# Two-layer hybrid decoder trunk: tile arithmetic taken off GpSimd, constant products ahead of x, short transposes gathered

## The chip, the cores and the metric

The kernel runs on one core of a Trainium2 chip. The metric is device time in microseconds (us) of one execution; the median of several runs counts. TensorE (PE) does the matmuls and transposes, VectorE (DVE), ScalarE (ACT) and GpSimd (POOL) the elementwise work, SyncE (SP) issues most DMAs. PSUM is the accumulator memory that matmuls write to, SBUF the working memory that everything else lies in.

## The reference, cut to what matters

Two layers over a sequence of 512 rows and 1024 channels, all in fp32, then a last RMSNorm.

```python
for l in range(2):
    h = rmsnorm(x, g_mix[l]); z = h @ w_in[l]          # columns split among the three mixers and the gates
    a = swa_mixer(...)     # sliding window 128, 8 heads, rotary positions, a learned sink per head
    b = nsa_mixer(...)     # 8 heads; compressed, selected and windowed keys, gated per head
    c = mla_mixer(...)     # 8 heads; low-rank q and kv ("latent"), rotary part of 32 channels
    m = sum(sigmoid(gate_i) * (mixer_i @ w_br[l, i]))  # merge
    x = x + m @ w_out[l]
    x = x + cross_attention(rmsnorm(x, g_x[l]), mem)   # 4 heads of 128, 256 memory rows
    h = rmsnorm(x, g_ffn[l])
    x = x + (silu(h @ w_gate) * (h @ w_up)) @ w_d[l]   # inner size 2816
out = rmsnorm(x, g_final)
# rope(u) = u * cos + swap(u) * sin ; rmsnorm(x) = x / sqrt(mean(x^2) + eps) * g
```

## The kernel before, in words

Activations lie with channels on partitions: x is 8 tiles of 128x512 (channels x sequence). A product in fp32 accuracy is three matmuls of TensorE in a faster type: each operand is split into a high part and a rest, and `mm3` multiplies high by high (L307), rest of x by high of w (L308), high of x by rest of w (L309). For the weights, ACT writes the high part `wh` from the loaded `wraw` (L246) and DVE the rest `wl` (`tt`, L166). For the activations, `norm_split` has ACT write `xh` (L175) and DVE `xl` (L176), both already multiplied by the norm's gain. Weights come in chunks of 512 KB; SP issues their DMAs ahead of their use into three `wraw` buffers, POOL some of those of the FFN's combined weights (`sum`).

**A norm.** `norm_begin` names an engine; `norm_tile` squares a tile on ACT (L336) and adds it into `acc` on the named engine, GpSimd unless told otherwise. `norm_end` sums `acc` over partitions with matmuls onto ones (L359), adds a last part (`end`, L361), takes the root on ACT and the reciprocal on DVE, spreads the result over partitions with one more matmul (L371) and copies it from PSUM into `rstd` (L374). A norm's factor is applied behind the product that uses x, in `evac` or where the result is read (`tmp<-mm,rstd`), so the product's matmuls don't wait for it.

**Rotary positions.** `rotate` multiplies the swapped halves by `sin` on GpSimd, the tile by `cos` on DVE and adds. `k_tiles` then copies the two heads of a key tile out to both halves of the partitions: four copies on ACT, four subtractions on DVE.

**Attention.** A `Half` is two blocks of 128 queries of one head (four in mixer A). `attend` runs all of them as one pipeline of steps, one block a step: scores of the new block on PE, its softmax on DVE and ACT, and, four steps later (`lags`), `turn`: its block of probabilities is transposed on PE into a PSUM tile `tp`, and split into `ph` (ACT, L172) and `pl` (DVE, L173). When both blocks of a Half are turned, `values` multiplies with v into the one PSUM bank `av` (`av_tile`, one buffer), and one step later `out_half` empties the bank: ACT copies one half of its partitions (L701), DVE adds the other to it. The step's PE work is woven with matmuls of the projections by `skew`, `weave` and `drain`, and the order on each engine is then set by the framework's scheduler. DVE and ACT work strictly in that order.

**Merge, FFN, end.** `merge_tasks` multiplies each mixer's projection with its gate and adds the three into `mg` on GpSimd. In the FFN, `sums` forms the operands of a scheme with seven products in place of eight; two of its four differences are on GpSimd. `final` multiplies x by gain and norm in one DVE instruction for each of 16 half tiles (`fin`, L1450), and SP sends each out by a DMA of its own (L1452).

Of the kernel before, what the change touches and what calls it, by code (L numbers as in the profile page):

```python
# [121 lines left out]
CUTS, W1, POS, SQP = 2, 4, 5, (1, 2, 3, 4)  # L122
# [24 lines left out]
class Trunk:  # L147
    def __init__(self, ctx, tc, a, plan):
# [3 lines left out]
        self.lags = (2, 4)  # L152
# [169 lines left out]
    def norm_begin(self, n=512, eng=None, pool=None):  # L322
        return {"n": n, "acc": None, "x": [], "eng": eng or self.nc.gpsimd, "pool": pool or self.sh}
# [27 lines left out]
    def norm_end(self, st, dim, out, pool=None, bank=None):  # L351
# [5 lines left out]
        for j in range(nb):  # L357
            c = slice(j * 128, j * 128 + 128)
            nc.tensor.matmul(ps[:, j:j + 1], acc[:, c], self.ones[:, 0:1], start=True, stop="end" not in st)  # L359
            if "end" in st:  # L360
                nc.tensor.matmul(ps[:, j:j + 1], st["end"][:, c], self.ones[:, 0:1], start=False, stop=True)  # L361
# [11 lines left out]
        r = (pool or self.sh).tile([128, n], F32, name="rstd", tag="rstd", bufs=1 if pool else 2)  # L373
        nc.scalar.copy(r, ps)  # L374
        out["r"] = r
# [11 lines left out]
    def consts(self):  # L387
        nc, sh = self.nc, self.sh
        self.gains = sh.tile([128, G_FINAL + 8], F32, name="gains")
        nc.sync.dma_start(self.gains, self.a["gains"])  # L390
# [4 lines left out]
        nc.vector.memset(self.ones, 1.0)  # L395
        self.ident = sh.tile([128, 128], F32, name="ident")
# [93 lines left out]
    def k_tiles(self, kr):  # L490
# [45 lines left out]
    def k_task(self, src, x, n, box, key):  # L536
# [7 lines left out]
        box[key] = self.k_tiles(self.rotate(f, s))  # L544
# [11 lines left out]
    class Half:  # L556
# [3 lines left out]
        def __init__(self, o, scores, blocks, mask, scale, value, after, av=None, pre=None, last=True, init=3e38,  # L560
                     sink=False, gate=None, band=False):
            self.o, self.scores, self.blocks, self.mask, self.scale = o, scores, blocks, mask, scale
            self.value, self.after, self.av, self.pre, self.last = value, after, av, pre, last
            self.init, self.sink, self.gate, self.band = init, sink, gate, band
            self.ks = sorted(set(b for bl in blocks for b in bl))
            self.p, self.ps, self.ext = {}, {}, {}

# [35 lines left out]
        def turn(self, i):  # L603

            o, bl = self.o, self.blocks[i]
            if i == 0:
# [3 lines left out]
            if self.band:  # L610
                c = slice(bl[0] * 256 + 128 * (len(bl) - 1), i * 256 + 128)
                o.split(*(t.rearrange("p b q -> p (b q)")[:, c] for t in (self.ph, self.pl)),
                        tp.rearrange("p b q -> p (b q)"))
                return 110 * len(bl)
            j = self.ks.index(bl[0])
            c = slice(i * 128, i * 128 + 128)
            o.split(self.ph[:, j:j + len(bl), c], self.pl[:, j:j + len(bl), c], tp)
            return 110 * len(bl)

        def values(self):  # L620
# [4 lines left out]
            if "ps" not in self.av:  # L625
                self.av["ps"] = self.o.av_tile(512 if self.band else 256)
            ps = self.av["ps"]
            cost = 0
# [4 lines left out]
            elif self.pre is None and self.av.get("begun"):  # L633
                first = False
            self.av["begun"] = True
# [13 lines left out]
            todo = [(w, self.ks.index(b), c, x) for b, c in todo for w, x in self.value(self, b)]  # L649
            for n, (w, b, c, x) in enumerate(todo):  # L650
                nc.tensor.matmul(ps[:, c], w, x[:, b, c], start=first and n == 0,
                                 stop=self.last and n == len(todo) - 1)
            return cost + 109 * len(todo)

    def attend(self, jobs):

        q, done, out = [], [], []
        ls, lt = self.lags

        def step(new):  # L660
            cost = 0
            if new is not None:
                cost += new[0].score(new[1])
            if len(q) > ls and q[-ls] is not None:
# [3 lines left out]
            if len(q) > lt and q[-lt] is not None:  # L668
                h, i = q[-lt]
                cost += h.turn(i)  # L670
                if i == len(h.blocks) - 1:
                    done.append(h)
# [19 lines left out]
        for _ in range(lt + 3):  # L692
            yield step(None)

    def out_half(self, of, av, g, half, n=256):
# [3 lines left out]
        c = slice(256 * half, 256 * half + n)  # L699
# [8 lines left out]
    def jobs_a(self, l, box, of):  # L708
# [13 lines left out]
        for t in range(4):  # L722
            yield lambda t=t: ("q", t) in box
            of.append(self.of_tile())
            for g in range(2):
# [4 lines left out]
                                lambda ps, o=of[t], g=g: self.out_half(o, ps, g, 0, 512),  # L730
# [118 lines left out]
    def jobs_b(self, b, of):  # L849
# [18 lines left out]
        for t in range(4):  # L868
            yield lambda t=t: ("pc", t) in b and ("q", t) in b
            of.append(self.of_tile())  # L870
            for g in range(2):
                h = t + 4 * g
                for half in range(2):
                    av = {}
                    blocks = [list(range(i + 1)) for i in (2 * half, 2 * half + 1)]
                    for br, k, v in ((1, "ks", "vs"), (2, "kw", "vw")):
# [4 lines left out]
                                        lambda ps, o=of[t], g=g, half=half: self.out_half(o, ps, g, half), av=av,  # L881
                                        pre=(lambda ps, t=t, g=g, half=half: add_cmp(ps, t, g, half)) if br == 1 else None,
                                        last=br == 2, gate=gate)
# [93 lines left out]
    def jobs_c(self, box, of):  # L977
# [14 lines left out]
        for h in range(8):  # L992
# [3 lines left out]
            v = box[h][2]  # L996
            for half in range(2):
# [3 lines left out]
                                lambda ps, o=of[h // 2], g=h % 2, half=half: self.out_half(o, ps, g, half))  # L1001
# [585 lines left out]
```

## Time and profile before

| | |
|---|---|
| median of 3 runs | 2030.93 us (2027.62 to 2031.45) |
| profiled execution | 2028.9 us, its span 2027.2 us |
| PE busy | 1977.0 us, 98% |
| DVE / ACT / POOL busy | 1392.9 / 1196.9 / 243.2 us |
| mean granted TensorE clock | 0.996 of full speed |

How to read it: PE is busy nearly all the time, so the interesting figures are the short stretches in which it is not. A row of the timeline is one instruction or a run of equal ones: its start, its time, the engine, the line, and in square brackets how long the engine had been idle before it and whose result it then took up. A stretch in which PE's idle time is ended by DVE shows a wait for VectorE, and the next question is what VectorE did instead. The program's stages by time are: 0 to 50 us the loads and the first norm, 50 to 330 mixers A and B, 330 to 500 the latent mixer C, 500 to 650 merge and cross attention, 650 to 720 the entry of the FFN, up to 1005 the FFN; the second layer repeats this 1000 us later and ends with the last norm at 2016 to 2027.

### The profile page before, as it was taken

Reading aid. Unit: us, or ns where it says so; the run is one execution under the profiler, and the core shown is the slowest. Engines: PE = TensorE matmul, PEld = TensorE weight load, DVE = VectorE, ACT = ScalarE, POOL = GpSimd, SP = SyncE. Lnnn points to the kernel's source line nnn. Section 1 sums busy time; section 2 is a strip of 40 time slices with the busy share of each in tenths; the row PEclk is TensorE's granted clock in tenths of the full one; section 3 lists DMA queues with packets and bytes.
Section 4 is the critical chain, followed back from the end, with each engine's and each line's share of the span. In section 5 each row is a group of like instructions: output and inputs, shape, how many; then the busy total and the mean of one; then the engine's idle time right before and its main releaser. Section 6 shows DMA issues by size and latency. Waiting matters only on the chain. (4 is left out here: it accounts for less than half of the span.)

```text
span 2027.2 us, 30844 instructions
## 1 busy us (share of the span) xinstructions
PE 1977.0 (98%) x11368; PEld 1689.5 (83%) x11368; DVE 1392.9 (69%) x2734; ACT 1196.9 (59%) x2408; POOL 243.2 (12%) x234
## 2 busy tenths in 40 slices
PE   7999999999999999999999999999999999999998
PEld 5778887878888798989877788877788878989897
DVE  7897777676557884757577977676654579657475
ACT  5787786875456562534456867877744565435252
POOL 2210001012211200100112100001022021001000
PEclk9999999999999999999999999999999999999999
DMA  6321212224332563745343222122333344647432
GB/s 190 105 79 58 68 48 89 73 84 130 102 104 75 159 177 114 183 121 140 116 120 106 64 66 63 54 86 76 111 110 104 105 117 116 167 135 194 116 106 69
DMA packets 85743, 218.00 MB, mean 108 GB/s; under 512 B 11208, under 2 KB 17096, under 8 KB 85592
## 3 DMA queue, kind: packets, MB, share of 16 engines
q1 hardware_dynamic: 75800, 197.16, 31.5%
q0 software_dynamic: 9792, 18.88, 5.8%
q8 instruction: 89, 1.46, 0.3%
q14 instruction: 62, 0.51, 0.1%
HBM read 200.23 MB, written 4.75 MB: 101 GB/s over the span
## 5 line engine op out<-in xcount | busy, mean ns | idle before, releaser
L246 ACT CAST wh<-wraw 128x1024 fp32r<-128x1024 f32 (+3 forms) x275 | 277.4, 1009 | 367.5 <-PE mm L308 239.9
L307 PE MATMUL mm<-xh,wh 128*128 128x512 f32 x928 | 384.4, 414 | 7.8 <-ACT wh L246 6.5
L166 DVE TENSOR_TENSOR wl<-wraw,wh 128x1024 fp32r<-128x1024 f32 (+3 forms) x275 | 334.7, 1217 | 71.1 <-ACT wh L246 66.4
L308 PE MATMUL mm<-xl,wh 128*128 128x512 f32 x928 | 373.6, 403 | 3.8 <-DVE xl L176 3.8
L309 PE MATMUL mm<-xh,wl 128*128 128x512 f32 x928 | 371.7, 401 | 4.1 <-DVE wl L166 4.1
L309 PEld LDWEIGHTS mm<-xh,wl 128*128 128x128 f32 x928 | 176.0, 190 | 45.7 <-DVE wl L166 6.5
L307 PEld LDWEIGHTS mm<-xh,wh 128*128 128x128 f32 x928 | 176.7, 190 | 41.1 <-ACT wh L246 7.0
L308 PEld LDWEIGHTS mm<-xl,wh 128*128 128x128 f32 x928 | 177.0, 191 | 39.4 <-DVE xl L176 6.7
L589 ACT ACTIVATE p<-p,st 128x256 f32<-128x256 f32 (+5 forms) x288 | 155.3, 539 | 49.0 <-DVE st L583 42.8
L166 DVE TENSOR_TENSOR x<-x,mm 128x512 f32<-128x512 f32 (+1 forms) x88 | 55.6, 637 | 154.2 <-PE mm L309 153.9
L173 DVE TENSOR_TENSOR pl<-tp,ph 128x256 fp32r<-128x256 f32 (+3 forms) x288 | 131.2, 457 | 43.7 <-ACT ph L172 41.1
L601 ACT ACTIVATE p<-p,st 128x256 f32<-128x256 f32 (+3 forms) x288 | 141.8, 532 | 20.3 <-DVE st L166 12.8
L172 ACT CAST ph<-tp 128x256 fp32r<-128x256 f32 (+3 forms) x288 | 113.1, 395 | 40.0 <-PE tp L519 37.9
L583 DVE CUSTOM_DVE_ANT_0 p<-s,causal 128x128 f32<-128x128 f32 (+2 forms) x224 | 106.2, 476 | 39.6 <-PE s L859 16.1
L519 PE MATMUL tp<-ident,p 128*128 128x128 f32 x656 | 122.3, 278 | 8.3 <-DVE v L173 2.9
L166 POOL TENSOR_TENSOR acc<-acc,tmp 128x512 f32<-128x512 f32 (+1 forms) x55 | 75.6, 1375 | 450.3 <-ACT tmp L336 292.0
L308 PE MATMUL mm<-h,wh 128*128 128x512 f32 x304 | 120.2, 396 | 0.0
L307 PE MATMUL mm<-h,wh 128*128 128x512 f32 x304 | 120.2, 395 | 0.0
L309 PE MATMUL mm<-h,wl 128*128 128x512 f32 x304 | 120.2, 395 | 0.0
L519 PEld LDWEIGHTS tp<-ident,p 128*128 128x128 f32 x656 | 78.1, 141 | 31.0 <-DVE pl L173 6.9
L266 POOL DMA_DIRECT2D sum<-in_w_gu x36 | 43.7, 1239 | 455.9 <-DMA sum<-in_w_gu 205.7
L166 POOL TENSOR_TENSOR mg<-mg,gt 128x512 f32<-128x512 f32 x32 | 48.0, 1501 | 359.5 <-DVE gt L1040 359.3
(299 smaller groups left out, 4961.5 us busy)
## 6 DMA issues: line engine op xcount, KB each, us to landing
wraw<-in_w_in SPq DMA_DIRECT2D x91, 512.0 KB, 3.6
wraw<-in_w_gu SPq DMA_DIRECT2D x52, 512.0 KB, 3.6
sum<-in_w_gu SPq DMA_DIRECT2D x36, 512.0 KB, 4.6
sum<-in_w_gu POOLq DMA_DIRECT2D x36, 512.0 KB, 5.8
wraw<-in_w_d SPq DMA_DIRECT2D x32, 512.0 KB, 3.8
wraw<-in_w_br SPq DMA_DIRECT2D x24, 512.0 KB, 3.6
up<-in_w_gu SPq DMA_DIRECT2D x36, 256.0 KB, 2.7
wraw<-in_w_xkv SPq DMA_DIRECT2D x16, 512.0 KB, 3.5
```

Source lines behind the costliest of these rows:

```text
L166: (eng or self.nc.vector).tensor_tensor(out=out, in0=a, in1=b, op=op)
L172: nc.scalar.copy(hi, src)
L173: (eng or nc.vector).tensor_tensor(out=lo, in0=src, in1=hi.bitcast(F32), op=OP.subtract)
L246: nc.scalar.copy(wh[:, j:j + n], raw[:, j:j + n])
L266: nc.gpsimd.dma_start(s, ends, accum_op=OP.add)
L307: nc.tensor.matmul(ps, wh[:, c], xh, start=i == 0, stop=False)
L308: nc.tensor.matmul(ps, wh[:, c], xl, start=False, stop=False)
L309: nc.tensor.matmul(ps, wl[:, c], xh, start=False, stop=i == len(blocks) - 1)
L519: self.nc.tensor.transpose(tp[:, j], src[:, j * 128:j * 128 + 128], self.ident)
L583: o.nc.vector.tensor_tensor_reduce(out=p, in0=self.ps.pop(i), in1=self.mask(self.blocks[i]), scale=-self.scale, scalar=self.init, op0=OP.a ...
L589: self.o.nc.scalar.activation(p, p, AF.Exp, scale=-1.0, bias=st[:, 0, i:i + 1], accum_out=st[:, 1, i:i + 1])
L601: nc.scalar.activation(self.p[j], self.p[j], AF.Copy, scale=self.st[:, 2, j:j + 1])
```

## The change

- All tile arithmetic that POOL did (121 instructions: 41 and 14 additions into `acc` of 128x512 and 128x256, 32 additions into `mg`, 22 products with `sin`, 8 FFN differences, 4 squares) goes to DVE, the 4 squares to ACT. POOL keeps masks, fills, small sink copies and DMA issues.
- A turn gathers more: where the two blocks of a Half have at most four key blocks together (mixer A, the first halves of B and C, cross attention), both are transposed into one `tp` and split at once, three steps behind the second one's scores. 192 splits of 128 to 512 columns on each of ACT and DVE become 96 of 384 or 512.
- The two halves of a head in B, C and cross attention share one `av` bank, which is emptied once: 64 additions of 64x256 become 32 of 64x512, with as many copies.
- In two `k_tiles` per layer the second placement is done by two SP DMAs in place of two copies and two subtractions.
- In the final norm x times gain is done by ACT as soon as x is there; behind the norm stands one DVE product for two tiles, which reads the norm from PSUM without the copy, and 8 DMAs of two tiles instead of 16.
- At the start: 11 matmuls of ones ahead, the gains' DMA on ACT's queue, `positions` behind the last x, one weight chunk later.

```diff
+CUTS, W1, WARM = 2, 5, 11
-        self.lags = (2, 4)
+        self.lags = (2, 3, 4)
 def norm_begin
-        return {..., "eng": eng or self.nc.gpsimd, ...}
+        return {..., "eng": eng or self.nc.vector, ...}
 def norm_end
-        for j in range(nb):
-            nc.tensor.matmul(ps[:, j:j + 1], acc[:, c], self.ones[:, 0:1], start=True, stop="end" not in st)
-            if "end" in st:
-                nc.tensor.matmul(ps[:, j:j + 1], st["end"][:, c], ...)
+        parts = [acc] + ([st["end"]] if "end" in st else [])
+        for i, a in enumerate(parts):
+            for j in range(nb):
+                nc.tensor.matmul(ps[:, j:j + 1], a[:, j * 128:j * 128 + 128], self.ones[:, 0:1], ...)
...
-        nc.scalar.copy(r, ps)
+        if keep:
+            nc.scalar.copy(r, ps)
+            ps = r
 def rotate
-        self.tt(s, s, self.sin, OP.mult, self.nc.gpsimd)
+        self.tt(s, s, self.sin, OP.mult)
 def k_tiles
+        if copied:
+            for g, m in enumerate(halves):
+                self.tt(k[m, 2 + g], kr[m], k[m, g].bitcast(F32), OP.subtract)
+                nc.sync.dma_start(k[halves[1 - g], g::2].bitcast(F32), k[m, g::2].bitcast(F32))
+            return k
 class Half
+            self.paired = all(len(blocks[i]) + len(blocks[i + 1]) <= 4 for i in range(0, len(blocks), 2))
 def turn
-            tp = o.tp4(self.p.pop(i), len(bl))
+            todo = [(k, j) for j in ((i - 1, i) if self.paired else (i,)) for k in self.blocks[j]]
+            for n, (k, j) in enumerate(todo):
+                o.nc.tensor.transpose(tp[:, n], self.p[j][:, c:c + 128], o.ident)
...
+                o.split(... [:, c:c + 128 * n] ...)
 def values
-                self.av["ps"] = self.o.av_tile(512 if self.band else 256)
+                self.av["ps"] = self.o.av_tile(512)
+                ps = ps[:, 256 * self.half:256 * self.half + 256]
 def step
-            if len(q) > lt and q[-lt] is not None:
-                cost += h.turn(i)
+            if q[-lt] is not None and not q[-lt][0].paired:
+                cost += turn(*q[-lt])
+            if q[-lp] is not None and q[-lp][0].paired and q[-lp][1] % 2:
+                cost += turn(*q[-lp])
...
-            if done and not (len(q) > lt and q[-lt] is not None and q[-lt][0] is done[0]):
+            if done:
...
+            done.extend(fresh)
 def out_half
-        self.nc.scalar.copy(t[m, :n], av[x])
-        self.tt(of[m, c], av[m], t[m, :n], OP.add)
+        self.nc.scalar.copy(t[m], av[x])
+        self.tt(of[m], av[m], t[m], OP.add)
 def merge_tasks
-                self.tt(m, m, t, OP.add, nc.gpsimd)
+                self.tt(m, m, t, OP.add)
 def sums
-            self.tt(f[0], b11, b12, OP.subtract, nc.gpsimd)
-            self.tt(f[2], b22, b12, OP.subtract, nc.gpsimd)
+            self.tt(f[0], b11, b12, OP.subtract)
+            self.tt(f[2], b22, b12, OP.subtract)
 def down_half (last layer)
+            nc.scalar.activation(fins[-1][:, i % n], xt[i][:, c], AF.Copy, scale=self.gains[:, g:g + 1])
 def final
-                nc.vector.scalar_tensor_tensor(t, xt[i][:, c], self.gains[:, g:g + 1], rh[half]["r"], ...)
-                nc.sync.dma_start(self.a["out"][:, i, c], t)
+                self.tt(f, f, rh[half]["r"][:, None, :].to_broadcast([128, 2, 256]), OP.mult)
+                nc.sync.dma_start(self.a["out"][:, i:i + 2, 256 * half:256 * half + 256], f)
 def build
-            if k == POS:
-                o.positions()
...
+        o.positions()
-            o.norm_tile(st, xs[k], nc.gpsimd if k in SQP else None)
+            o.norm_tile(st, xs[k])
```

The change moves instructions on the engines' queues. On DVE where the FFN of the first layer is entered (the last tiles of x come from the cross attention's projection, `xl` is the rest of x for the FFN, `wl` that of a weight chunk, `acc` the norm's sum), before:

```order
L166 TENSOR_TENSOR x_5137<-x_5137,mm 128x512
L166 TENSOR_TENSOR wl<-wraw,wh 128x1024
L176 SCALAR_TENSOR_TENSOR xl_6916<-x_5137,gains,xh_6915 128x512
L166 TENSOR_TENSOR x_5139<-x_5139,mm 128x512
L176 SCALAR_TENSOR_TENSOR xl_6943<-x_5139,gains,xh_6942 128x512
L166 TENSOR_TENSOR x_5141<-x_5141,mm 128x512
L166 TENSOR_TENSOR wl<-wraw,wh 128x1024
L176 SCALAR_TENSOR_TENSOR xl_6951<-x_5141,gains,xh_6950 128x512
L166 TENSOR_TENSOR wl<-wraw,wh 128x1024
L365 RECIPROCAL sd<-sd 128x4
```

And the same place of the changed kernel:

```order
L176 SCALAR_TENSOR_TENSOR xl_6704<-x_4961,gains,xh_6703 128x512
L166 TENSOR_TENSOR acc<-acc,tmp 128x512
L166 TENSOR_TENSOR x_4963<-x_4963,mm 128x512
L166 TENSOR_TENSOR x_4965<-x_4965,mm 128x512
L166 TENSOR_TENSOR wl<-wraw,wh 128x1024
L176 SCALAR_TENSOR_TENSOR xl_6731<-x_4963,gains,xh_6730 128x512
L166 TENSOR_TENSOR acc<-acc,tmp 128x512
L176 SCALAR_TENSOR_TENSOR xl_6739<-x_4965,gains,xh_6738 128x512
L166 TENSOR_TENSOR acc<-acc,tmp 128x512
L166 TENSOR_TENSOR wl<-wraw,wh 128x1024
L365 RECIPROCAL sd<-sd 128x4
```

The three additions into `acc` stand in DVE's row, which POOL did beside it, the last two of them one before and one behind the last `xl`. The second place is DVE's queue at the start, where the first norm's sum is ready (`rope` are the tables of the rotary positions). Before:

```order
L166 TENSOR_TENSOR acc<-acc,tmp 128x512
L436 TENSOR_SCALAR rope_187<-rope_187 128x512
L166 TENSOR_TENSOR wl<-wraw,wh 128x1024
L438 SCALAR_TENSOR_TENSOR rope_186<-rope_187,rope_186 128x512
L365 RECIPROCAL sd<-sd 128x4
L166 TENSOR_TENSOR wl<-wraw,wh 128x1024
```

After:

```order
L166 TENSOR_TENSOR acc<-acc,tmp 128x512
L444 SCALAR_TENSOR_TENSOR rope_198<-rope_199,rope_198 128x512
L166 TENSOR_TENSOR acc<-acc,tmp 128x512
L444 SCALAR_TENSOR_TENSOR rope_198<-rope_199,rope_198 128x512
L365 RECIPROCAL sd<-sd 128x4
L166 TENSOR_TENSOR wl<-wraw,wh 128x1024
```

The weight's `wl` that stood ahead of the reciprocal (which waits for PE and ACT) now stands behind it, and additions into `acc` alternate with the tables. The third place is PE's queue in the latent attention, from the last value product of a head (`av<-pl`) on (`mm` projections, `s` scores, `tp` transposes of probabilities). Before:

```order
L651 MATMUL av<-pl,v 128x128
L307 MATMUL mm<-oh,wh 128x512
L308 MATMUL mm<-oh,wh 128x512
L309 MATMUL mm<-oh,wl 128x512
L986 MATMUL s<-k,q 128x256
L987 MATMUL s<-k,q 128x256
L988 MATMUL s<-k,q 128x256
L519 MATMUL tp<-ident,p 128x128
L307 MATMUL mm<-oh,wh 128x512
L308 MATMUL mm<-oh,wh 128x512
L309 MATMUL mm<-oh,wl 128x512
L307 MATMUL mm<-oh,wh 128x512
```

After:

```order
L674 MATMUL av<-pl,v 128x128
L307 MATMUL mm<-oh,wh 128x512
L308 MATMUL mm<-oh,wh 128x512
L309 MATMUL mm<-oh,wl 128x512
L307 MATMUL mm<-oh,wh 128x512
L308 MATMUL mm<-oh,wh 128x512
L628 MATMUL tp<-ident,p 128x128 x3
L309 MATMUL mm<-oh,wl 128x512
L1014 MATMUL s<-k,q 128x256
L1015 MATMUL s<-k,q 128x256
L1016 MATMUL s<-k,q 128x256
L674 MATMUL av<-ph,v 128x256
```

Before, ten more matmuls and transposes follow the rows shown until the next product into `av` starts; in the changed kernel it starts in the last row shown, after 12.

## Rows read from the trace of the kernel before

**Rows 1.** The page: span, and busy time of each engine.

```profile
span 2027.2 us, 30844 instructions
PE 1977.0 (98%) x11368; PEld 1689.5 (83%) x11368; DVE 1392.9 (69%) x2734; ACT 1196.9 (59%) x2408; POOL 243.2 (12%) x234
```

**Rows 2.** Busy time by stretches; columns in the first line.

```profile
core 0: us, PE busy (x) PEld busy (x) DVE busy (x) ACT busy (x) POOL busy (x), PEclk, DMA share, GB/s
0.00:50.00 50.00, 39.27 (x156) 29.05 (x156) 38.55 (x61) 25.35 (x37) 13.61 (x21) 1.00 0.62 189
50.00:330.00 280.00, 273.62 (x1545) 227.02 (x1544) 219.02 (x588) 212.98 (x519) 27.85 (x40) 1.00 0.24 71
330.00:500.00 170.00, 165.73 (x829) 134.05 (x828) 116.71 (x233) 120.96 (x262) 22.35 (x19) 1.00 0.32 99
650.00:720.00 70.00, 67.39 (x320) 54.74 (x319) 59.60 (x76) 36.98 (x56) 18.14 (x13) 0.98 0.50 135
720.00:1005.00 285.00, 285.00 (x1926) 262.61 (x1925) 178.24 (x255) 127.65 (x185) 23.54 (x19) 1.00 0.53 143
1050.00:1500.00 450.00, 438.30 (x2345) 360.94 (x2344) 332.08 (x806) 331.47 (x775) 49.66 (x59) 1.00 0.27 81
1650.00:1720.00 70.00, 66.58 (x316) 53.97 (x316) 58.42 (x75) 36.82 (x55) 15.92 (x12) 0.98 0.49 134
666.30:669.70 3.40, 3.40 (x10) 2.72 (x11) 2.10 (x3) 1.86 (x3) 0.62 (x1) 0.50 1.11 236
```

**Rows 3.** Groups of POOL: line, operation, count | busy us, mean ns | idle before.

```profile
L166 POOL TENSOR_TENSOR acc<-acc,tmp 128x512 f32<-128x512 f32 (+1 forms) x55 | 75.6, 1375 | 450.3 <-ACT tmp L336 292.0 <-PE mm L308 132.5 <-issue 25.1
L166 POOL TENSOR_TENSOR mg<-mg,gt 128x512 f32<-128x512 f32 x32 | 48.0, 1501 | 359.5 <-DVE gt L1040 359.3
L166 POOL TENSOR_TENSOR tmp<-tmp,sin 128x512 f32<-128x512 f32 x22 | 31.8, 1444 | 257.7 <-DVE st L597 72.0 <-DMA tmp<-qf 64.1 <-DMA tmp<-tmp 54.4
```

**Rows 4.** Instructions on tile xl: ns minimum/median/maximum, first to last start.

```profile
L176 DVE SCALAR_TENSOR_TENSOR xl<-x,gains,xh x40: 742/746/1779, 539.5 to 1662.0; 128x512 fp32r<-128x512 f32 x40
```

**Rows 5.** Groups by shape, DVE and ACT: count | busy us, mean ns | idle before.

```profile
L166 DVE TENSOR_TENSOR acc<-acc,tmp 128x512 f32<-128x512 f32 x7 | 4.8, 683 | 0.1
...
L166 DVE TENSOR_TENSOR of<-av,tmp 64x512 f32<-64x512 f32 x16 | 11.0, 687 | 4.3 <-ACT tmp L701 3.7
...
L701 ACT COPY tmp<-av 64x512 f32<-64x512 f32 x16 | 9.3, 580 | 1.3 <-PE av L642 0.9
```

**Rows 6.** Timeline, FFN entry of layer 0: start, us, instruction, idle before.

```profile
663.04 1.35 POOL L166 TENSOR_TENSOR acc<-acc,tmp 128x512 f32<-128x512 f32 x1 [0.85 <-ACT tmp L336]
663.19 1.75 DVE L176 SCALAR_TENSOR_TENSOR xl<-x,gains,xh 128x512 fp32r<-128x512 f32 x1
...
664.99 0.50 PE L308 MATMUL mm<-xl,wh 128*128 128x512 f32 x1 [1.67 <-DVE xl L176]
```

**Rows 7.** Timeline, FFN entry of layer 1.

```profile
1678.72 1.21 DVE L166 TENSOR_TENSOR wl<-wraw,wh 128x1024 fp32r<-128x1024 f32 x1
1679.99 0.78 PE L309 MATMUL mm<-xh,wl 128*128 128x512 f32 x1 [1.52 <-DVE wl L166]
```

**Rows 8.** Timeline, latent attention of layer 0, two of PE's waits.

```profile
348.27 0.50 PE L309 MATMUL mm<-xh,wl 128*128 128x512 f32 x1 [0.66 <-DVE wl L166]
...
443.62 0.33 PE L519 MATMUL tp<-ident,p 128*128 128x128 f32 x1 [1.02 <-DVE v L173]
```

**Rows 9.** Timeline, start of mixer A: PE's wait for rotated queries.

```profile
49.67 0.33 PE L717 MATMUL s<-k,q 128*128 128x128 f32 x1 [1.55 <-DVE q L166]
```

**Rows 10.** Timeline, the end.

```profile
2019.76 0.37 ACT L374 COPY rstd<-av 128x256 f32<-128x256 f32 x1 [2.03 <-PE av L371]
2020.16 3.25 DVE L1450 SCALAR_TENSOR_TENSOR fin<-x,gains,rstd 128x256 f32<-128x256 f32 x8 [1.78 <-ACT rstd L374]
2020.67 3.77 SPq L1452 DMA_DIRECT2D out_dram<-fin  x8
```

**Rows 11.** Timeline, DVE beside the first norm's sum.

```profile
23.69 1.22 DVE L166 TENSOR_TENSOR wl<-wraw,wh 128x1024 fp32r<-128x1024 f32 x1
```

More of the change, by code (lines that the diff above doesn't have):

```diff
@@ L349, in norm_split, with norm_end @@
         st["x"].append((h, lo))
-    def norm_end(self, st, dim, out, pool=None, bank=None):
+    def norm_end(self, st, dim, out, pool=None, bank=None, keep=True):
         nc, n = self.nc, st["n"]
@@ L395, in consts @@
         nc.vector.memset(self.ones, 1.0)
+        ps = self.av_tile(128)
+        for _ in range(WARM):
+            nc.tensor.matmul(ps, self.ones, self.ones, start=True, stop=True)
         self.ident = sh.tile([128, 128], F32, name="ident")
@@ L632, in values @@
                 first = False
-            elif self.pre is None and self.av.get("begun"):
+            elif self.av.get(self.half):
                 first = False
-            self.av["begun"] = True
+            self.av[self.half] = True
             todo = []
@@ L648, in values @@
                 todo += [(b, slice(i * 128, i * 128 + 128)) for b in bl if b not in both]
[L649 to L652, printed above, removed]
+            todo = [(w, self.ks.index(b), c, slice(0, 128) if self.paired and b not in both else c, x)
+                    for b, c in todo for w, x in self.value(self, b)]
+            for n, (w, b, c, cx, x) in enumerate(todo):
+                nc.tensor.matmul(ps[:, c], w, x[:, b, cx], start=first and n == 0,
+                                 stop=self.end and n == len(todo) - 1)
             return cost + 109 * len(todo)
@@ L657, in attend, with turn @@
         q, done, out = [], [], []
-        ls, lt = self.lags
+        ls, lp, lt = self.lags
         def step(new):
-            cost = 0
+            cost, fresh = 0, []
+            def turn(h, i):
+                if i == len(h.blocks) - 1:
+                    fresh.append(h)
+                return h.turn(i)
             if new is not None:
                 cost += new[0].score(new[1])
-            if len(q) > ls and q[-ls] is not None:
+            if q[-ls] is not None:
                 q[-ls][0].norm(q[-ls][1])
@@ L691, in attend, with out_half @@
                 yield step((job, i))
[L692 removed]
+        for _ in range(lt + 4):
             yield step(None)
[L695 removed]
+    def out_half(self, of, av, g):
         m = slice(64 * g, 64 * g + 64)
         x = slice(64 - 64 * g, 128 - 64 * g)
[L699 removed]
         t = self.tmp()
[L701 to L702 removed]
+        self.nc.scalar.copy(t[m], av[x])
+        self.tt(of[m], av[m], t[m], OP.add)
     def of_tile(self):
@@ L880, in jobs_b @@
                                         lambda u, bb, g=g, v=v: [(b[v][:, g, bb], u.ph), (b[v][:, g, bb], u.pl)],
-                                        lambda ps, o=of[t], g=g, half=half: self.out_half(o, ps, g, half), av=av,
+                                        lambda ps, o=of[t], g=g: self.out_half(o, ps, g), av=av,
                                         pre=(lambda ps, t=t, g=g, half=half: add_cmp(ps, t, g, half)) if br == 1 else None,
-                                        last=br == 2, gate=gate)
+                                        last=br == 2 and half == 1, gate=gate, half=half, end=br == 2)
     def latent_task(self, l, x, n, st, fs, t):
@@ L1000, in jobs_c @@
                                 lambda u, b, v=v: [(v[:, b], u.ph), (v[:, b], u.pl)],
-                                lambda ps, o=of[h // 2], g=h % 2, half=half: self.out_half(o, ps, g, half))
+                                lambda ps, o=of[h // 2], g=h % 2: self.out_half(o, ps, g), av=av, last=half == 1,
+                                half=half)
     def merge_tasks(self, l, x, n, br, of, done=None):
@@ L1220, in value, with after @@
             return [(v[:, 0, b], u.ph), (v[:, 0, b], u.pl), (v[:, 1, b], u.ph)]
-        def after(ps, h, half):
-            c = slice(half * 256, half * 256 + 256)
-            if h not in os:
-                os[h] = xa.tile([128, 2, 512], F32R, name="xos", tag="xq", bufs=4)
-            self.split(os[h][:, 0, c], os[h][:, 1, c], ps)
+        def after(ps, h):
+            os[h] = xa.tile([128, 2, 512], F32R, name="xos", tag="xq", bufs=4)
+            self.split(os[h][:, 0], os[h][:, 1], ps)
         def jobs():
@@ L1233, in jobs @@
                                     lambda u, b, h=h: value(u, b, h),
-                                    lambda ps, h=h, half=half: after(ps, h, half))
+                                    lambda ps, h=h: after(ps, h), av=av, last=half == 1, half=half)
             yield lambda: 3 in mem["v"]
```

84 lines of the change are left out of this document (45 added, 39 removed).

## The prediction

> **What bounds the kernel now.** I read the page's busy times first: PE 1977.0 of a span of 2027.2 us [rows 1]. TensorE's work is the bound, and the change leaves it as it is but for 11 warm-up matmuls ahead of the first load; gathering transposes doesn't make them fewer. So what can be won is PE's idle time, 2027.2 − 1977.0 = 50.2 us, and the stretches in which its clock is low. The table by stretches says where that lies [rows 2]: 10.7 us in the first 50; 6.4 in mixers A and B of the first layer, 4.3 in its latent attention, 11.7 in both of the second layer; 2.6 and 3.4 at the two entries of the FFN; nothing at all in the FFN behind (285.00 busy of 285). [...]
>
> Then the releasers: which instruction ended each of PE's longer waits, and what that engine's neighbours did. At the FFN entry PE waits 1.67 us for the last `xl`; that DVE instruction took 1.75 us, while POOL added into `acc` from 663.04 to 664.39 [rows 6]. The same operation on tile `xl` has a median of 746 ns and a maximum of 1779 [rows 4]. An instruction of DVE with two operands in SBUF more than doubles while POOL's arithmetic runs. That is the pattern I look for, since POOL's arithmetic goes: 75.6 us of `acc`, 48.0 of `mg`, 31.8 of `sin` [rows 3].
>
> **The change part by part**, against the profiled execution of 2028.9 us (span 2027.2, 1.7 around it; the median, 2030.93, is 2.0 above).
>
> *FFN entries, −7.* First layer: without POOL's addition the last `xl` takes 0.75 instead of 1.75, and the one before it likewise, so PE's 1.67 goes. The moved additions stand between the `xl`s in DVE's row (the order shows one between the last two): 0.68 each [rows 5]. By pairs of tiles, DVE has two x additions, a `wl` of 1.22, two `xl` of 0.75 and two `acc`, some 5.1 us, beside 24 matmuls of PE at 67.39/320 = 0.21 mean [rows 2], 5.1, somewhat more since shorter ones are in that mean: it fits, narrowly. With the idle goes the clock's fall: 1.67 + 1.7 = 3.4. Second layer: idle 3.4 in all, of which 1.52 ended with a `wl` behind the norm's chain [rows 7], and again 1.7 of clock: 5.1. Together 8.5. I take 7, because the second wait hangs on a chain of DMA, ACT and DVE that loses its contention but no link. Bounds: −8.5, and +1 if the three additions in the row only make `xl` late by other means.
>
> *Latent attention, −4.4.* The waits of 0.66 and 1.02 us [rows 8] are ended by a `wl` and by `v`, each behind a DVE instruction that ran beside POOL's `mg` (1.50 each [rows 3]). I take half of the 4.3 idle there, 2.2 a layer; bounds 0 and −8.6. The `mg` addition on DVE costs 0.68 in its queue, not on PE; DVE is busy 117 of 170 [rows 2] there, so nothing waits for it longer than that.
>
> *Rotary part, −3.* PE's 1.55 us for rotated queries [rows 9] stand behind four `k` subtractions and POOL's product of 1.44 us mean [rows 3]; on DVE the product is 0.68, without the handover. One such wait a layer; bounds 0 and −6.
>
> *Gathered turns and emptyings, −2.* 96 splits and 32 emptyings fewer on each of ACT and DVE (elements the same, so only each instruction's start is saved), 8 subtractions and copies fewer. Of the 22.4 idle in attention [rows 2] some 15 are left after the two terms above; DVE is busy 219 of 280 in mixers A and B, and that gets lighter. Bounds −8 and +6: a paired turn comes with four blocks at once, three steps behind.
>
> *The shared `av` bank, +2.* It is emptied once per head in one go, 0.58 on ACT, then 0.69 on DVE [rows 5], with the semaphores about 1.5 us. In PE's queue 12 instructions lie between the last product of one head and the first of the next; 165.73/829 = 0.20 us mean [rows 2] makes that 2.4 us, where 21 instructions, 4.2 us, lay before. What hides it is the projection work woven between; if DVE has another 0.7 of work ahead, it is short. 16 such handovers a layer. Bounds 0 and +32 (below).
>
> *FFN differences, −0.5.* 8 on DVE in place of POOL: nothing in the FFN proper, where PE doesn't idle [rows 2]; of the 2.6 us at the first entry 0.9 is left over the 1.67, and half of it is taken. Bounds −0.9 and +1.
>
> *The end, −1.8.* The copy of 0.37 goes, 8 `fin` in 3.25 and 8 DMA issues in 3.77 become 4 and 4 of double size [rows 10]. The last issue was at 2024.04 (2020.67 + 3.77, less its own); four products of 512 columns at 0.68 from about 2019.4 are through at 2022.2, an issue behind each, and the landing stays as it was. Bounds −2.5 and −0.5.
>
> [...]
>
> *The head, +1.* `acc` is now added by DVE between the rope tables: seven additions of 0.68 there in place of POOL's. The order puts a `wl` that ran beside the norm's sum (23.69, 1.22 us [rows 11]) behind the reciprocal, which waits for PE and ACT. On the other side `xl`s without contention come sooner. Followed by hand the two give +0.5, and a fall of the clock may be added. Bounds −3 and +3.
>
> Sum: −7 − 4.4 − 3 − 2 + 2 − 0.5 − 1.8 + 1 = −15.7, 2028.9 − 15.7 = 2013.2. The runs of before spread over 3.8 us with the profile in the lower half, so I put the median at 2014.
>
> **The rivals.**
>
> *The waits move.* DVE has the additions in its own row; where PE waited for an `xl` slowed by POOL, it waits for an `xl` behind an `acc` of 0.68. For it: at the FFN entry DVE is busy 59.6 of 70 [rows 2], and 5.1 of little more than 5.1 by hand. Against it: what the contention added to one `xl` (1.0) is more than one addition. Half of the FFN, latent and rotary terms would be left: 14.4/2 = 7.2 less, 2021.
>
> *The `av` handover decides: slower.* In NSA and latent attention, the first product of a head waits for the emptied bank, and `out_half`'s addition stands in DVE's strict row behind softmax work and the moved `mg`. If each of 32 handovers costs PE 1.0 us, that is 32, not 2: 2043. It decides from about (15.7 + 2)/32 = 0.55 us a handover. For it: 2.4 us of cover against 1.5, with DVE 78% busy in mixers A and B [rows 2]. Against it: the order has the add two or three places behind the copy, and the longest work that can stand there is one addition or split of 0.7.
>
> *DVE becomes the bound.* 117 instructions at 0.68 are up to 80 us more on 1392.9 [rows 1], minus the splits and the contention that go. In mixers A and B that would be 219 plus about 13 (the POOL share of 27.85 at half its duration): 232 of 280, 83%, still short of PE's; worth 10 us at most, 2023, and counted with the first rival.
>
> *More is won.* The attention stages lose most of the 15 us left, and the head 3: below 2004.
>
> **How the numbers follow.** Forecast 0.58, its own range 2005 to 2021. Waits move or DVE fills up, around 2022, 0.22, a third of it above 2026.9. More is won 0.07. The handover 0.10. Nothing of the kind, that the time stays within a few us, 0.03. A measurement here tells about 0.2% (4 us) from no change: faster is below 2026.9, slower above 2035. Faster: 0.58 + 0.15 + 0.07 + 0.02 of the handover's mild end = 0.82; same 0.09; slower 0.09. The range 2002 to 2028 leaves out the far ends of the last cases.
>
> **What would show it.** In the profile after: no arithmetic of POOL, and no `xl` on DVE above 0.8 us; the two FFN entries with a clock of 1.00 and under 1 us idle; PE idle in all some 37 us; 4 `fin` products at the end, and the last issue some 2 us sooner behind the last product for x. Against me: waits of PE at the first `av` product of a head ended by `of<-av,tmp`, in the order of 0.5 us and more, or PE idle at the FFN entries ended by an `acc` or a `wl` behind one; DVE above 85% in mixers A and B.

## The result and the profile after

The changed kernel takes 2001.61 us (median of 4 runs, 1999.6 to 2002.22) against 2030.34: ratio 0.986, 95% interval 0.9844 to 0.9875, 28.7 us less. Forecast were 2014 and a range of 2002 to 2028; the direction was right, the time lies 0.4 us below the range, and the gain is almost twice what the sum gave. Of the attention pipeline the sum made nothing, where undoing it costs 11.0 us; the address of an operand, worth 6.6, wasn't in it.

The page after, to be read against [rows 1]:

```profile
span 2000.1 us, 30439 instructions
PE 1965.3 (98%) x11390; PEld 1691.0 (85%) x11390; DVE 1400.3 (70%) x2699; ACT 1187.7 (59%) x2282; POOL 70.1 (4%) x113
```

PE's idle time went from 50.2 to 34.8 us, near the 37 that I had expected; but PE's *busy* time fell as well, by 11.7 us, for the same matmuls and the 11 of the warm-up, which the page counts as 22. Of that the prediction had only the two falls of the clock at the FFN entries, by its estimate 3.4 us. To place the rest, both spans are cut at the same events (first attention scores, first merged product, first product of cross attention's output, first combined product of the FFN, `s<-T,S24h`). Before, both attention stretches, both stretches with an FFN entry, and the first FFN:

```profile
49.70:531.70 482.00, 471.35 (x2534) 388.09 (x2535) 351.81 (x840) 346.05 (x796) 56.26 (x63) 1.00 0.28 83
625.20:714.60 89.40, 86.33 (x410) 69.27 (x411) 71.70 (x115) 53.16 (x100) 20.36 (x14) 0.98 0.42 115
714.60:1043.40 328.80, 328.80 (x2141) 298.74 (x2140) 207.42 (x295) 147.26 (x214) 32.76 (x30) 1.00 0.52 142
1043.40:1530.50 487.10, 475.00 (x2553) 391.79 (x2553) 353.65 (x841) 347.30 (x797) 55.88 (x63) 1.00 0.28 83
1624.00:1714.30 90.30, 86.42 (x409) 69.16 (x410) 71.40 (x115) 53.10 (x100) 19.24 (x14) 0.98 0.42 114
```

And after, with the head:

```profile
0.00:50.00 50.00, 42.31 (x174) 32.46 (x174) 36.56 (x63) 27.51 (x41) 9.69 (x15) 0.93 0.63 193
50.00:524.00 474.00, 467.48 (x2535) 387.94 (x2536) 352.46 (x815) 338.56 (x736) 8.54 (x28) 1.00 0.29 86
617.60:702.20 84.60, 81.29 (x399) 66.62 (x399) 67.38 (x113) 52.26 (x93) 2.57 (x2) 1.00 0.39 111
702.20:1031.90 329.70, 329.70 (x2148) 300.23 (x2146) 214.11 (x307) 147.44 (x214) 20.21 (x22) 1.00 0.53 144
1031.90:1510.40 478.50, 471.88 (x2554) 391.21 (x2554) 354.58 (x816) 339.48 (x737) 7.55 (x28) 1.00 0.30 87
1603.90:1687.20 83.30, 81.20 (x400) 66.68 (x400) 67.48 (x113) 52.34 (x93) 2.40 (x2) 1.00 0.39 112
```

Attention gives 8.0 and 8.6 us, the FFN entries 4.8 and 7.0, at clock 1.00 instead of 0.98; the head gives nothing. The FFN behind is 0.9 and 1.6 us longer, as some matmuls moved behind the cut (2148 in the first, 2141 before), so entry and FFN together give 3.9 and 5.4. In the attention stretches idle time is only part of the gain (10.7 to 6.5, 12.1 to 6.6); the rest, 3.9 and 3.1 us, is matmuls that follow each other faster. The groups of the product over x show it. Before, then after:

```profile
L307 PE MATMUL mm<-xh,wh 128*128 128x512 f32 x928 | 384.4, 414 | 7.8 <-ACT wh L246 6.5
L308 PE MATMUL mm<-xl,wh 128*128 128x512 f32 x928 | 373.6, 403 | 3.8 <-DVE xl L176 3.8
L309 PE MATMUL mm<-xh,wl 128*128 128x512 f32 x928 | 371.7, 401 | 4.1 <-DVE wl L166 4.1
```

```profile
L307 PE MATMUL mm<-xh,wh 128*128 128x512 f32 x928 | 376.9, 406 | 3.4 <-ACT wh L246 2.0
L309 PE MATMUL mm<-xh,wl 128*128 128x512 f32 x928 | 366.0, 395 | 4.8 <-DVE wl L166 4.7
L308 PE MATMUL mm<-xl,wh 128*128 128x512 f32 x928 | 367.1, 396 | 0.3 <-DVE xl L176 0.3
```

Each of these 2784 matmuls is 6 to 8 ns shorter. From start to start (for `xh`, mean of the gaps under 260 ns in the first layer, so without waits) it is 233.8 ns before and 229.1 after. The products over `h`, `mo` and `oh` don't move: 233.3, 233.3 and 233.1 before, 233.3, 233.3 and 233.0 after. So it is neither the clock nor the chip of the day.

### The profile page after: what moved, and what is told of

Its sections match the earlier page's. It is cut to its first block, busy times and chain, and to the rows that moved or that the text cites. A ratio compares the mean times of both kernels' runs of the same rounds, so it can differ in the third digit from the quotient of the medians.

```text
span 2000.1 us, 30439 instructions
## 1 busy us (share of the span) xinstructions
PE 1965.3 (98%) x11390; PEld 1691.0 (85%) x11390; DVE 1400.3 (70%) x2699; ACT 1187.7 (59%) x2282; POOL 70.1 (4%) x113
## 4 chain that ended last, share of the span: by engine, by line
PE 80%; DVE 8%; ACT 7%; DMA 2%; issue 2%; SPq 0%; POOL 0%; DVEq 0%; ACTq 0%
PE mm L307 17%; PE mm L309 17%; PE mm L308 17%; PE s L294 10%; PE tp L294 5%; PE av L674 3%; PE tp L628 3%; PE av L294 3%; ACT p L614 2%; ACT p L602 1%; DVE wl L166 1%; DMA sum<-in_w_gu 1%; ACT wh L246 1%; DVE p L596 1%; ACT ph L172 1%
## 5 line engine op out<-in xcount | busy, mean ns | idle before, releaser
L307 PE MATMUL mm<-xh,wh 128*128 128x512 f32 x928 | 376.9, 406 | 3.4 <-ACT wh L246 2.0
L309 PE MATMUL mm<-xh,wl 128*128 128x512 f32 x928 | 366.0, 395 | 4.8 <-DVE wl L166 4.7
L166 DVE TENSOR_TENSOR wl<-wraw,wh 128x1024 fp32r<-128x1024 f32 (+3 forms) x275 | 322.7, 1174 | 64.2 <-ACT wh L246 61.2
L308 PE MATMUL mm<-xl,wh 128*128 128x512 f32 x928 | 367.1, 396 | 0.3 <-DVE xl L176 0.3
L173 DVE TENSOR_TENSOR pl<-tp,ph 128x384 fp32r<-128x384 f32 (+1 forms) x192 | 116.7, 610 | 42.5 <-ACT ph L172 41.6
L172 ACT CAST ph<-tp 128x384 fp32r<-128x384 f32 (+1 forms) x192 | 98.7, 517 | 37.1 <-PE tp L628 35.1
L628 PE MATMUL tp<-ident,p 128*128 128x128 f32 x656 | 110.9, 277 | 4.8 <-DVE v L173 2.2
L307 PE MATMUL mm<-oh,wh 128*128 128x512 f32 x192 | 79.4, 413 | 0.0
L309 PE MATMUL mm<-oh,wl 128*128 128x512 f32 x192 | 76.7, 399 | 0.0
```

Source lines behind the costliest of these rows:

```text
L166: (eng or self.nc.vector).tensor_tensor(out=out, in0=a, in1=b, op=op)
L172: nc.scalar.copy(hi, src)
L173: (eng or nc.vector).tensor_tensor(out=lo, in0=src, in1=hi.bitcast(F32), op=OP.subtract)
L307: nc.tensor.matmul(ps, wh[:, c], xh, start=i == 0, stop=False)
L308: nc.tensor.matmul(ps, wh[:, c], xl, start=False, stop=False)
L309: nc.tensor.matmul(ps, wl[:, c], xh, start=False, stop=i == len(blocks) - 1)
```

## The experiments

Three theories: *contention* (GpSimd's arithmetic slowed DVE, and PE waited), *address* (the edit that moves `positions` behind the splits of x also moves the tiles `xh` and `xl`, from byte 50400 of a partition to 35904, and TensorE reads them faster there), *turns* (the gathered transposes and emptyings relieve DVE and ACT where attention waits). A rival to the second is *traffic*: matmuls go faster because GpSimd no longer uses SBUF. The median of before in these comparisons is 2028.9 to 2029.4, in that of the changed kernel 2030.3. What an edit costs the changed kernel is a difference between two comparisons, so it is no sharper than some 1.5 us.

**GpSimd's arithmetic alone.** The kernel before with `nc.gpsimd` replaced in the five places.

```diff
-"eng": eng or self.nc.gpsimd              # and rotate, merge_tasks, sums (2), the squares
+"eng": eng or self.nc.vector
```

> The kernel before with GpSimd's tile arithmetic alone moved (acc, mg, sin and FFN differences to VectorE, the four squares to ScalarE); order of loads, turns, av bank, end and all addresses as before. My prediction's terms for this part (FFN entries -7, latent attention -4.4, rotary -3, FFN differences -0.5): 2030.3 - 15 = 2015 us, PE idle some 38 us. Traffic theory: also the 12 us of matmul pace, about 2003. Rival (the waits only move into VectorE's row): 2023 or more.

2018.53 us, ratio 0.9943 (0.9926 to 0.996): 10.6 us. Matmuls over `xh` at 233.8 ns: the traffic theory is out. From the first product of cross attention's output to the next layer's first scores, or to the end, the run is 3.7 and 4.1 us shorter, with clock 1.00 at the entries; I had taken 7.5 for entries and differences. Attention gave −1.4 (slower) and 3.1, where I had taken 7.4. Of the waits I had named there, those for `q` (1.9 to 0.35 us over both layers) and for `wl` (1.3 to nothing) did go. The one for `v` stayed, 1.4 us a layer before; in the first layer of this run:

```profile
PE tp L519 <- DVE v L173: 1.3, 2, 0.9
```

And new ones came, in the timeline of this run; the same two were under 0.2 us before:

```profile
334.16 0.73 PE L307 MATMUL mm<-lat,wh 128*128 128x512 f32 x2 [1.13 <-ACT lat L175]
335.02 2.07 DVE L176 SCALAR_TENSOR_TENSOR lat<-lf,gains,lat 128x512 fp32r<-128x512 f32 x3
335.82 0.79 PE L308 MATMUL mm<-lat,wh 128*128 128x512 f32 x1 [0.93 <-DVE lat L176]
```

**And put back into the changed kernel.**

```diff
+self.tt(m, m, t, OP.add, nc.gpsimd)       # and acc, sin and the FFN differences
```

> The changed kernel with acc, mg, sin and the FFN differences back on GpSimd (117 instructions; the squares stay on ScalarE), all else as changed. Additive with what moving them alone gave in the kernel before (10.6): 2012 us, at the two FFN entries the clock at half for 3.4 us again. If gathered turns and GpSimd's arithmetic cover for each other, less than half of it: under 2007. If DVE, relieved by 96 splits, only now has room for the additions: more, 2015 or above.

2017.31 us (0.994, 0.9925 to 0.9955): 15.7 us. One `xl` takes up to 1789 ns again; after, none:

```profile
L176 DVE SCALAR_TENSOR_TENSOR xl<-x,gains,xh x40: 743/747/1789, 537.5 to 1651.9; 128x512 fp32r<-128x512 f32 x40
```

```profile
L176 DVE SCALAR_TENSOR_TENSOR xl<-x,gains,xh x40: 739/746/749, 531.9 to 1639.6; 128x512 fp32r<-128x512 f32 x40
```

So GpSimd's arithmetic costs 10.6 us in the kernel before and 15.7 in the changed one. Of the 15.7, 9.9 lie in the attention stretches (479.5 and 482.9 us in place of 474.0 and 478.5), where moving it alone had given 1.7; the clock fell at the second FFN entry alone (0.98). That DVE has room for the additions since it has fewer splits would fit, but is not shown: the changed kernel differs in more than that, and no run has the two edits alone together.

**The attention pipeline as before.** `Half`, `attend`, `out_half` and the job lists of before in the changed kernel.

> The changed kernel with the attention pipeline of the kernel before: single turns four steps behind, 192 splits, av bank emptied after each half; all else as changed, all addresses as changed. My prediction's terms (gathered turns and emptyings -2, av bank +2, together 0): 2001.6, no change. Rival, since GpSimd's part measured alone gave 10.6 us and the address of xh 6.6 of the 28.7: the gathered turns give most of the 11.5 left, so undoing them costs 8 to 10: 2010 us, PE idle up by as much between 50 and 520 us and between 1030 and 1510.

2012.64 us (0.9921, 0.9904 to 0.9937): 11.0 us, 9.8 by the spans of the profiled executions (2009.9 and 2000.1). The attention stretches are 478.6 and 483.0 us long with 11.6 and 11.7 idle. Then only the pairing undone:

```diff
-            self.paired = all(len(blocks[i]) + len(blocks[i + 1]) <= 4 for i in range(0, len(blocks), 2))
+            self.paired = False
```

> The changed kernel with every block turned by itself four steps behind its scores (192 splits as before); the av bank stays shared by the two halves and emptied once. Undoing both cost 11.0. If the gathering of turns is the gain: 2011, and the shared bank is worth 0 to 1. If the shared bank (32 emptyings less, one start of a bank less) is the gain: 2003. My prediction's terms (-2 and +2) would have it 2003.6.

2006.07 us (0.9885, 0.9871 to 0.99): 4.5 us, 3.4 by span. The remaining 6.5 belong to the shared bank and the order of steps that goes with it, which no run separates; it is the edit that I had put down at +2. The waits of PE in the first layer's attention (in total, times, longest), before, then after:

```profile
PE tp L519 <- DVE pl L173: 1.6, 4, 0.6
PE s L717 <- DVE q L166: 1.6, 1, 1.6
PE tp L519 <- DVE v L173: 1.4, 2, 1.0
...
PE av L642 <- DVE pl L173: 0.8, 1, 0.8
...
PE mm L309 <- DVE wl L166: 0.7, 1, 0.7
```

```profile
PE tp L530 <- ACT tmp L973: 1.2, 1, 1.2
PE tp L628 <- DVE v L173: 1.1, 2, 0.8
...
PE av L674 <- DVE pl L173: 0.5, 2, 0.3
...
PE s L745 <- DVE q L166: 0.2, 1, 0.2
PE av L893 <- DVE of L166: 0.2, 1, 0.2
```

Over both layers, PE's waits for `pl` are 5.9 us before, 6.9 with the old pipeline in the changed kernel, 3.3 without pairing, 0.9 after. The last row is the handover that my slower rival was made of: 0.2 us.

**The address of xh.** One small tile allocated ahead of `xh` instead of behind moves `xh` and `xl` by 32 bytes and nothing else:

```diff
+        o.freq = o.sh.tile([128, 4], F32, name="freq")
         for k in range(KT):
             o.norm_split(st, xs[k], k, G_MIX)
```

> The changed kernel with one tile of 16 bytes allocated ahead of the xh and xl tiles instead of behind them: their addresses move by 32 bytes, from a multiple of 64 to 32 beyond one (where they lay before the change); no instruction and no other address changes. Address theory (a matmul reads its moving operand faster from a multiple of 64 bytes; 2784 matmuls over xh and xl, 233.7 ns each before, 229.0 after): 2001.6 + 13 = 2015 us, mean of the L307 group over xh back from 406 to about 414 ns, PE's idle time as after (35 us). Traffic theory (the matmuls go faster because GpSimd no longer uses SBUF beside them): 2001.6, 406 ns.

2008.2 us (0.9891, 0.9876 to 0.9906): 6.6 us. From its page:

```profile
PE 1976.0 (98%) x11390; PEld 1691.8 (84%) x11390; DVE 1400.8 (70%) x2699; ACT 1188.7 (59%) x2282; POOL 69.7 (3%) x113
L307 PE MATMUL mm<-xh,wh 128*128 128x512 f32 x928 | 381.2, 411 | 2.3 <-ACT xh L175 1.6
```

No instruction differs; the 2784 matmuls follow each other at 233.1 in place of 229.1 ns. PE is busy 10.7 us longer (1976.0 − 1965.3), but not all of that is the address. Head and attention of this run, to be read against the rows after:

```profile
0.00:50.70 50.70, 45.74 (x174) 35.31 (x174) 36.54 (x63) 27.63 (x41) 9.68 (x15) 0.87 0.63 191
50.70:527.50 476.80, 470.60 (x2536) 388.10 (x2536) 352.63 (x815) 338.67 (x736) 8.27 (x28) 1.00 0.29 85
1035.10:1516.40 481.30, 474.85 (x2553) 391.11 (x2553) 354.57 (x816) 339.72 (x737) 7.34 (x28) 1.00 0.29 86
```

In the head PE is busy 3.4 us longer at a granted clock of 0.87 in place of 0.93, and idle 2.7 us less. In attention it is busy 3.1 and 3.0 us longer, its idle time hardly moves (6.5 to 6.2, 6.6 to 6.5), and the two stretches are 2.8 us longer each: 5.6 of the 6.6 us. With the edit itself in the kernel before:

> The kernel before with the one edit that moves the xh tiles: positions (and so its tiles) behind the last split of x. Addresses of all tiles are then those of the changed kernel (xh0 at 35904, 64 beyond a multiple of 128; before 50400, 96 beyond one). Address theory: matmuls over xh and xl at 229 ns in place of 233.7, as in the changed kernel, 2029 - 7 (what the address was worth in the run with xh moved back) = 2022 us or lower, with the head's own change of -3 to +3 in it. Rival (the pace comes from the changed order of work, the address only goes along): 233.7 ns and 2029.

2028.42 us, ratio 0.9998 (0.9988 to 1.0007): 229.4 ns, and no gain at all. In the profiled execution (2031.42, the longest of ten) the head is 3.2 us longer; in attention PE is busy 0.8 and 2.9 us less and idle 2.3 and 0.9 more. So in the kernel before most of what the pace gives there is waited away again; that DVE and ACT don't keep up with it is my reading, no run tests it.

Which addresses are fast? Padding of 32 bytes either side of `xh` in the kernel before:

> The kernel before with 32 bytes of padding ahead of the xh tiles and 32 behind xl7: xh and xl begin at multiples of 64 bytes, all else as before but for a shift by 64. Address theory: 2030.3 - 13 = 2017 us, PE busy 1977 down by some 12, idle time still about 50. Traffic theory: 2030, no change.

2023.93 us (0.9971, 0.996 to 0.9983), `xh` at 233.0: between the theories and no proof of either. "A multiple of 64" is not the rule. Of its 5.2 us, 3.7 lie in the stretches from the FFN's first combined product on. There the products over `xh` and `xl` have 256 columns. One of their groups, before, then in this run:

```profile
L294 PE MATMUL s<-xh,wh 128*128 128x256 f32 x144 | 40.7, 283 | 0.0
```

```profile
L294 PE MATMUL s<-xh,wh 128*128 128x256 f32 x144 | 39.9, 277 | 0.0
```

From start to start (gaps under 150 ns, both layers) the 432 products over x into `s` take 119.8 and 114.4 ns, the 432 into `av` 118.9 and 113.8, the 432 into `tp` 115.2 and 117.8: by estimate 3.5 us less. All operands of the changed kernel at 64, and at 0:

```diff
+        pad0 = o.sh.tile([128, 8], F32, name="pad0")      # behind xl7; in the second run 64 bytes ahead of xh too
```

> The changed kernel with 32 bytes of padding behind xl7, so that the moving operands of the other products (h, oh, mo, lat, xos, T and so on), which lie 32 beyond a multiple of 64, begin at multiples of 64 too. Address theory: 2268 matmuls of 512 columns over those tiles at 233.3 ns go to about 229: 2001.6 - 10 = 1991 us, and lower if the matmuls of 256 columns gain as well. Traffic theory: 2001.6, no change.

> The changed kernel with padding of 64 bytes ahead of the xh tiles and 32 behind xl7: xh, xl, h, oh, mo, lat, xos and T all begin at multiples of 128 (xh at 35968; 64 beyond one in the changed kernel, h at 32 beyond one). If multiples of 64 are fast: h and mo at 227 ns, xh at 229, total 1994 as in the run with all at 64. If only 64 beyond a multiple of 128 is fast (xh at a multiple of 128 in the padded kernel before stayed at 233.0): h and mo stay at 233.3, xh goes to 233, total 2008.

1993.98 us (0.9821, 0.9806 to 0.9836) and 1994.89 (0.9833, 0.9817 to 0.985): the first is the fastest kernel here, 7.6 us under the changed one for 32 bytes of padding. Products over `h`, before and with all at 64:

```profile
L307 PE MATMUL mm<-h,wh 128*128 128x512 f32 x304 | 120.2, 395 | 0.0
```

```profile
L307 PE MATMUL mm<-h,wh 128*128 128x512 f32 x304 | 118.3, 389 | 0.0
```

A kernel with each `xh` pair at another address, two with moved weights:

> The changed kernel with 32 bytes of padding ahead of xh1 to xh6 each: xh0 and xl0 begin 64 bytes beyond a multiple of 256, the pairs behind it at 96, 128, 160, 192, 224, 0 and 0. The pace of the matmuls over each pair is read from their starts. Padding by 64 (multiples of 64 fast): pairs 0, 2, 4, 6 and 7 at 229 ns or less, 1, 3 and 5 at 233. Phase in 128 (only 64 beyond a multiple of 128 is fast, since the padded kernel before with xh at a multiple of 128 stayed at 233.0): pairs 0 and 4 fast, the rest at 233. Phase in 256: pair 0 alone. Total some 2001.6 + 4 to 6.

> The changed kernel with 64 bytes of padding ahead of the weight buffers and 64 behind them: wraw, wh and wl begin at multiples of 128 (64 beyond one before), xh and xl stay 64 beyond a multiple of 128. If the phase of the moving operand alone counts: matmuls over xh at 229 ns, 2001.6. If moving operand and weights must have the same phase (the next weights are loaded while a matmul reads its operand): 233 ns, about 2008, as in the run with xh moved by 32.

> The changed kernel with 192 bytes of padding ahead of the weight buffers: wraw, wh, wl and xh, xl all begin at multiples of 256 (64 beyond one before), h and mo at 224 beyond one. So far xh stayed at 233.0 ns at a multiple of 256 with weights 64 beyond one (in the padded kernel before), and ran at 229 wherever both had the same phase. If the phase between moving operand and weights counts: 229 ns over xh, 2001.6. If the moving operand's own phase in 256 counts: 233 ns, 2008.

2008.4 and 2003.96 us (one run each), and 2001.05 (0.9856, 0.984 to 0.9873). In the ladder the pairs lie between 230.7 and 233.7 ns (the three products of a pair together), the first fastest and none at 229: that is the pattern of none of the three rules. It mixes addresses in neighbouring matmuls, and decides nothing. The others decide. Start addresses modulo 256 from the built programs, pace from starts as above:

| kernel | weights | xh | difference | ns | h | difference | ns |
|---|---|---|---|---|---|---|---|
| before | 64 | 224 | 160 | 233.8 | 32 | 224 | 233.3 |
| changed | 64 | 64 | 0 | 229.1 | 32 | 224 | 233.3 |
| xh moved by 32 | 64 | 96 | 32 | 233.1 | 32 | 224 | 233.3 |
| before, positions late | 64 | 64 | 0 | 229.4 | 32 | 224 | 233.3 |
| before, xh padded | 64 | 0 | 192 | 233.0 | 96 | 32 | 233.3 |
| all at 64 | 64 | 64 | 0 | 229.4 | 64 | 0 | 226.8 |
| all at 0 | 64 | 128 | 64 | 229.8 | 128 | 64 | 228.9 |
| weights moved by 64 | 128 | 192 | 64 | 229.9 | 160 | 32 | 233.3 |
| weights and xh moved by 192 | 0 | 0 | 0 | 229.1 | 224 | 224 | 233.3 |

`xh` at 0 is slow with weights at 64 and fast with weights at 0: for these products of 512 columns the pace goes with the difference between the two tiles' addresses, not with either address. 0 is fastest, 64 nearly so, 32, 160, 192 and 224 cost 4 to 7 ns a matmul. That 192 is slow, and with it that a multiple of 64 isn't enough, rests on one kernel, before with `xh` padded, which has GpSimd's arithmetic in it; but so has before with `positions` late, at 229.4. And the difference is not the whole rule: at 0 it is 229.1 ns over `xh` and 226.8 over `h`, and the products of 256 columns into `s` go another way, 119.7 ns at 0 (changed), 114.4 at 192, and at 64 both 113.8 (all at 0) and 117.8 (weights moved by 64). The reason no run shows.

## Why the prediction was wrong

*PE's work stays as it is, and 50.2 us idle is what can be won.* This step failed. The busy time held 2784 matmuls over x that were 4.7 ns slower from start to start by their operands' address (233.8, then 229.1); no view names addresses, but the diff moves an allocation, and I read that edit as order alone. Worth 6.6 us (undone), not in the sum.

*Gathered turns and emptyings −2, shared bank +2.* The largest miss, in size and, for the bank, in sign: 11.0 undone together, 4.5 of it pairing. I priced the bank by its handover (1.5 us against 2.4 of cover). That one emptying for two halves also takes away every second start of a bank, and half the copies and additions (for 64 additions of 422 ns come 32 of 688), I left out. PE's waits for `pl` fall from 6.9 to 3.3 us with the bank's edit and to 0.9 with the pairing; which part of it gives the rest of the gain stays open. The slower rival, 1.0 us at each of 32 handovers, met 0.2 us of waiting in a layer.

*Latent attention −4.4, rotary −3, FFN entries −7, differences −0.5.* Contention was there (`xl` at most 754 ns, 1779 before; clock 1.00 at both entries, 0.98 before), and the sum of 14.9 lies between 10.6 alone and 15.7 in company; but that it came so near is in part luck, as its division was off. Alone, the edit gave 7.8 from the entries on and 1.7 in attention, in place of 7.5 and 7.4. In attention the wait for `q` comes in the first layer alone, and I had counted it in both; the waits for `v` stayed (in the first layer 1.4 us before, 1.3 with GpSimd's arithmetic gone alone, 1.1 in the changed kernel), and ahead of the one in [rows 8] DVE had itself idled 0.35 us for ACT's half of `v`; and other waits stood ready (`lat`). At the entries I had expected under 1 us of idle time; it is 3.1 and 3.9 before, 3.3 and 2.1 after. The wait of 1.67 for `xl` went, and a `wl` took its place in the first layer and stayed in the second, 1.5 us each, as the rival had it, but no fall of the clock followed (1.00 from 668 to 675 us and from 1653 to 1660). No run shows the 1.7 us of clock that the sum has for each entry: before, the clock was 0.50 for 3.4 us at each (the first in [rows 2], the second from 1680.0 to 1683.5), and in the second stretch products of 512 columns over x started 0.425 us apart in place of 0.234; 3.4 × (1 − 0.234/0.425) makes an estimated 1.5 us. The first layer after:

```profile
669.32 0.49 PE L307 MATMUL mm<-xh,wh 128*128 128x512 f32 x1 [1.22 <-ACT wh L246]
...
670.29 1.21 DVE L166 TENSOR_TENSOR wl<-wraw,wh 128x1024 fp32r<-128x1024 f32 x1
...
671.56 0.50 PE L309 MATMUL mm<-xh,wl 128*128 128x512 f32 x1 [1.51 <-DVE wl L166]
```

*The end −1.8.* Right. From the last x tile to the end 11.6 us before, 10.0 after; these are the rows that answer to [rows 10]:

```profile
1993.52 2.48 DVE L166 TENSOR_TENSOR fin<-fin,av 128x512 f32<-128x512 f32 x4 [0.85 <-PE av L371]
1994.29 2.15 SPq L1485 DMA_DIRECT2D out_dram<-fin  x4
```

*The head +1.* Near: +0.3. PE arrives early and waits for `acc`, then for the `wl` behind the reciprocal, which answers to [rows 11]; the clock fell behind them (0.57 from 24 to 32 us). Of the first 50 us PE is 3.0 more busy, with the warm-up in it, and 3.0 less idle:

```profile
23.10 1.02 PE L360 MATMUL av<-ones,acc 128*128 128x1 f32 x8 [2.03 <-DVE acc L166]
24.46 0.18 DVE L365 RECIPROCAL sd<-sd 128x4 f32<-128x4 f32 x1 [0.90 <-ACT sd L364]
24.55 1.21 DVE L166 TENSOR_TENSOR wl<-wraw,wh 128x1024 fp32r<-128x1024 f32 x1
...
25.82 0.80 PE L309 MATMUL mm<-xh,wl 128*128 128x512 f32 x1 [1.70 <-DVE wl L166]
```

*DVE becomes the bound.* No: 70% busy, 69% before (1400.3 us for 1392.9, 1420.4 with the additions alone); what GpSimd handed over came back as splits (131.2 to 116.7 us), emptyings (38.0 to 33.0) and contention saved. *More is won* (0.07) is where the number fell, but not by its mechanism: it had most of 15 us of idle time in attention and 3 us of the head. Attention lost 9.6 us of idle time, the head no time at all, and the rest is the pace of matmuls and the FFN entries. I gave the terms of attention no joint chance of being much larger.

The pieces undone one by one (11.0 + 15.7 + 6.6) make 33.3, more than 28.7: they overlap, and at least some pay more with the others in place.

## What to carry to other kernels

A busy engine is not at its peak (98% busy here both at 233.8 ns a matmul and at 229.1): where PE is busy nearly all the time, compare the start-to-start pace of equal matmuls over different tiles, and look at tile addresses when a diff moves an allocation. Price a change in a pipeline by all that its engines no longer do ahead of the late result, not by the one handover that it adds. And a gain measured alone (10.6) can be half as large again beside other edits (15.7).

## What was not expected of the hardware

In these kernels the pace of a matmul of 512 columns goes with where its moving operand begins against the weights (start addresses taken modulo 256 bytes): over `h` 226.8 ns at no difference, 228.9 at 64 bytes, 233.3 at 32 or 224. Products of 256 columns have another order (into `s` 119.7 ns at none, 114.4 at 192).

VectorE's `xl` was not always slower beside GpSimd's arithmetic. Of the 40 over x before, 8 took 1743 to 1779 ns, each beside additions into `acc` on GpSimd for 1.2 us or more; 27 others that ran beside such an addition for 0.12 to 0.65 us took 742 to 752. With GpSimd's work put back the maximum is 1789 (median 747), in the changed kernel 749.
